# Small 32x32 products in the last step of a block inversion, and a later load of modulation weights

## The chip, the cores and the metric

The kernel runs on one core of a Trainium2 chip. The metric is device time in microseconds (us) of one execution, in which all weights are read from HBM.

## What is computed

The reference is a two-layer encoder trunk on 256 tokens of width 1024. Each layer has three sub-layers, each with a shift, a scale and a gate that are computed from a conditioning vector `c` (nine vectors of 1024 per layer, numbered 0 to 8 below):

```
for l in range(DEPTH):
    mod = cs @ ada_w[l] + ada_b[l]
    sh1, sc1, gt1, sh2, sc2, gt2, sh3, sc3, gt3 = jnp.split(mod, N_MOD, axis=-1)
    x = x + 0.5 * gt1 * swiglu(modulate(rmsnorm(x), sh1, sc1), ffn_wi[l, 0], ffn_wo[l, 0])
    x = x + gt2 * hybrid_mixer(modulate(rmsnorm(x), sh2, sc2), ...)
    x = x + 0.5 * gt3 * swiglu(modulate(rmsnorm(x), sh3, sc3), ffn_wi[l, 1], ffn_wo[l, 1])
```

The mixer has three branches of 8 heads of width 64: a dilated attention, a neighbourhood attention, and an RWKV-7 scan that runs once forward and once backward over the tokens. One step of the scan is

```
sa = jnp.einsum("dbhvk,dbhk->dbhv", state, a_vec)
state = state * w[..., None, :] + sa[..., None] * b_vec[..., None, :] + v[..., None] * k[..., None, :]
y = jnp.einsum("dbhvk,dbhk->dbhv", state, r)
```

## The kernel before, in words

**Dense products.** Every float32 weight tile is split into a high and a low part (ScalarE, line 374; VectorE, line 383), and each product of a 128x128 weight tile with 256 tokens is three matmuls (lines 418 to 420). This dense work is one thread of the program and goes on through all stages.

**The scan.** The tokens are cut into 4 chunks of 64, for both directions at once. Step n of `scan()` treats chunk n of the forward and chunk 3-n of the backward direction. Inside a chunk the recurrence becomes a triangular 64x64 system for each head and direction, and `invert()` computes its inverse (`TT`, and `T`, its transpose within 32x32 blocks). Two threads of `invert` run, one for chunks 0 and 2, one for 1 and 3; at most two chunks are held at a time, and a slot is given back when a step of the scan ends. For each chunk `invert` makes the products `pG` (line 1189), inverts the 8x8 diagonal blocks (`blocks8`: one matmul at line 1257, and 14 small VectorE operations at lines 1262 and 1266 between larger ones, the last at line 1269), and then joins blocks of 8, 16 and 32 in three levels. One level is: 16 products of 64x64 by 64x64 into `pX` (line 1213), a copy to SBUF (lines 863 or 865, on ScalarE or VectorE), 16 more into `pT` (line 1225), and a masked copy of the new corner blocks into `TT` (line 1227). After the levels 0 and 1 a VectorE transpose of 32x32 blocks (`flip`, line 1274) renews `T`. In the profile each of these float32 matmuls has two records, so 16 products are 32 records.

**After the scan.** Four `post` threads normalise its result, the last two write `oC` (lines 1486 to 1492), and the dense thread goes on with the product of `oC` and the third branch's weights, then with `w_out`.

**Modulations.** One block of the nine vectors (128 of their values) is a 512 KB load `araw` (issued by SyncE, line 509) and one VectorE multiply and sum over 128x1024 elements (line 482). When the dense work of FFN 1 has been ordered, `main` spawns the 24 blocks of the vectors 5, 7 and 6 with `ada(..., PACE, START)`: block i is loaded no earlier than START + PACE*i us later, by the planner's clock. They are read when `w_out` begins and in the next FFN.

**The order of the work.** No engine's order is written by hand. A planner (`Order`) runs all threads against a model of the engines, with a duration named at each `yield on(...)`, and emits the instructions in the order in which its model starts them; a changed duration or due time can move any instruction behind it. On the chip each engine then takes its instructions in that order. SBUF tiles come from a pool of 36 buffers, PSUM from 8 banks, and a thread that takes one waits until it is free.

Of the kernel before, what the change touches and what calls it, by code (L numbers as in the profile page):

```python
# [28 lines left out]
WARM = 0  # L29
NJ0 = 8  # L30
NXF, NXM = 4, 8
PACE, START = 7, 110
FPACE, FSTART = 5, 12
WPRIO = -1
LAT, MM = {"PE": 0.2, "ACT": 0.15, "DVE": 0.13, "SP": 0.0}, 0.329
# [122 lines left out]
def on(eng, dur, lat=None, tab=None):  # L158
    return ("on", eng, dur, LAT[eng if isinstance(eng, str) else eng[0]] if lat is None else lat, tab)


def wait(ev):
    return ("wait", ev, 0, 0)
# [6 lines left out]
def take(sem, n=1):  # L170
    return ("take", sem, n, 0)


def vec_t(n):
    return 0.07 + 1.04e-3 * n


def vec2_t(n):
    return 0.08 + 0.53e-3 * n


def act_t(n):
    return 0.05 + 0.83e-3 * n


def skew(a, b):

    return bass.AP(tensor=a.tensor, offset=a.offset, ap=[list(a.ap[0]), [b.offset - a.offset, 2]] + [list(x) for x in a.ap[1:]])
# [3 lines left out]
def trunk(ctx, tc, A, out):  # L192
    nc = tc.nc
    V, S_, P = nc.vector, nc.scalar, nc.tensor
# [7 lines left out]
    od = Order()  # L202
    s_raw, s_spl, s_ada = Sem(NRAW), Sem(NSPL), Sem(NADA)
    s_pm, s_px, s_big = Sem(NPM), Sem(8 - NPM), Sem(NBIG)
# [3 lines left out]
    def pmain():  # L208
        return ps.tile([128, 2, 256], F32, name="pmain", tag="bank", bufs=8)

    def paux(name, shape=(128, 512)):
        return ps.tile(list(shape), F32, name=name, tag="bank", bufs=8)

    def big(name, shape=(128, 4, S), dt=F32):
        return act.tile(list(shape), dt, name=name, tag="b4", bufs=NBIG)
# [7 lines left out]
    def free_big(n=1):  # L223
        od.release(s_big, n)
# [40 lines left out]
    for q in range(2):  # L265
        p = paux("pc")
# [7 lines left out]
    lvl = const.tile([128, 3, 2, 128], U8, name="lvl")  # L274
# [54 lines left out]
    for l in range(L):  # L329
# [3 lines left out]
        w = A["w_in"][l]  # L333
        gb = A["w_gb"][l]
        parts = {"a": (w, 8, 14), "b": (w, 14, 20), "c": (w, 0, 8), "A": (gb, 0, 6), "B": (gb, 6, 12), "g": (gb, 12, 16)}
        for q in ORDER:
            t, b0, b1 = parts[q]
# [498 lines left out]
    def half(h):  # L836
        return slice(64 * (h % 2), 64 * (h % 2) + 64)
# [22 lines left out]
    def copy_any(dst, src, n, f32=False):  # L860
        yield on(("ACT", "DVE"), (act_t(n), vec2_t(n) if f32 else vec_t(n)))
        if od.cur.pick == "ACT":
            S_.copy(dst, src)
        else:
            V.tensor_copy(dst, src)

    def mixer(l, st):
# [55 lines left out]
        def ar_view(d, q):  # L923
            return AR[d][q].rearrange("p (a b) t -> p a b t", a=2)
# [237 lines left out]
        def toks(c):  # L1162
            return slice(c * 64, c * 64 + 64)

        def invert(ns):
            for e in e_ab:
                yield wait(e)
            for n in ns:
                cs = (n, 3 - n)
                if n > 0:  # L1170
                    yield wait(e_got[n - 1])
                yield take(s_ck)
                for _ in range(3 + (n == ns[0])):
                    yield take(s_big)
                od.set(e_got[n])
                if n == ns[0]:
                    tx = big("tx", (128, 2, 2, 4, 64))
                    T, X = tx[:, 0], tx[:, 1]
                G = [big("G", (128, 2, 4, 128)) for _ in range(2)]
                tw = big("tw", (128, 2, 2, 4, 64))  # L1180
                TT, W1 = tw[:, 0], tw[:, 1]
                for d in range(2):
                    yield take(s_px, 2)
                    pp = [paux("pG", (128, 4, 128)) for _ in range(2)]
                    yield on("PE", 1.3)
                    for i in range(4):
                        for b in range(2):
                            hs = half(b)
                            P.matmul(pp[b][:, i], BK[d][i // 2][hs, i % 2, cs[d]].rearrange("p a b -> p (a b)"),  # L1189
                                     ar_view(d, i // 2)[hs, :, i % 2, toks(cs[d])], start=True, stop=True)  # L1190
                    for b in range(2):
                        yield on("DVE", 0.6)
                        V.tensor_mul(G[b][:, d], pp[b], mg[:, d][:, None, :].to_broadcast([128, 4, 128]))
                        od.release(s_px)
                yield from blocks8(G, X, TT)
                yield on("DVE", 0.6)
                flip(T, TT)
                od.spawn(values(n, cs, G, TT, W1), VPRIO)
                for lv in range(3):
                    w = 8 << lv  # L1200

                    def part_(t, d, a):
                        return t[:, d].rearrange("p h c -> p (h c)").rearrange("p (x a s) -> p x a s", a=2, s=w)[:, :, a]

                    def halves_(t, a):
                        return skew(part_(t, 0, a), part_(t, 1, 1 - a))

                    yield take(s_px)
                    px = paux("pX", (128, 2, 4, 64))
                    yield on("PE", 0.85)  # L1210
                    for d in range(2):
                        for h in range(8):
                            P.matmul(px[half(h), d, h // 2], G[h % 2][half(h), d, h // 2, 0:64], T[half(h), d, h // 2],  # L1213
                                     start=True, stop=True)
                    if lv == 0:
                        yield from copy_any(X, px, 512)
                    else:
                        yield from copy_any(halves_(X, 0), halves_(px, 0), 256)
                    od.release(s_px)
                    yield take(s_px)  # L1220
                    pt = paux("pT", (128, 2, 4, 64))
                    yield on("PE", 0.85)
                    for d in range(2):
                        for h in range(8):
                            P.matmul(pt[half(h), d, h // 2], X[half(h), d, h // 2], TT[half(h), d, h // 2], start=True, stop=True)  # L1225
                    yield on("DVE", 0.335)
                    V.copy_predicated(halves_(TT, 1), lvl[:, lv].rearrange("p d (x s) -> p d x s", s=w), halves_(pt, 1))
                    od.release(s_px)
                    if lv < 2:
                        yield on("DVE", 0.6)  # L1230
                        flip(T, TT)
                od.set(e_inv[n])
            free_big()

        def blocks8(G, m, TT):

# [35 lines left out]
        def flip(t, tt):  # L1272

            V.transpose(t.rearrange("p d a b -> p (d a b)"), tt.rearrange("p d a b -> p (d a b)"))
# [520 lines left out]
        for m in range(KT):  # L1795
            if m < NPM:
                p = p3[m]
                yield from dense(p, ma, KT, 4)
            else:
                yield take(s_pm)  # L1800
                p = pmain()[:, 0]
# [14 lines left out]
    def main():  # L1816
        st = first
        od.spawn(first_stats(st), -2)
        od.spawn(first_loads(), 0)
        od.spawn(late_consts(), 8)  # L1820
        od.spawn(weights(), WPRIO)
        od.spawn(weights_hi(), WPRIO)
        od.spawn(weights_lo(), WPRIO)
        for l in range(L):
            st = yield from ffn(l, 0, 0, st, [(l, 2), (l, 4), (l, 3)], (l, 1))
            od.spawn(ada([(l, 5), (l, 7), (l, 6)], 9, PACE, START), 9)
            st = yield from mixer(l, st)
            st = yield from ffn(l, 1, 2, st, [(l, 8), (l + 1, 1), (l + 1, 0)],
                                (l + 1, 0) if l + 1 < L else None)
        yield from rstd(st)  # L1830
        for k in range(KT):
            yield on("DVE", 0.34)
            V.tensor_mul(xT[:, k], xT[:, k], st.r)
            if k % 2 == 1 or k > 5:
                k0 = k - 1 if k < 6 else k
                nc.sync.dma_start(out[:, k0:k + 1], xT[:, k0:k + 1])
# [126 lines left out]
```

## Time and profile before

| | before |
|---|---|
| median of 3 runs | 1553.74 us (1552.37 to 1556.83) |
| profiled execution | 1554.94 us, span 1553.1 us |
| TensorE busy | 1508.4 us of the span (97%) |
| VectorE busy | 1282.1 us (83%) |
| ScalarE busy | 870.0 us (56%) |
| mean granted TensorE clock | 0.984 |

Busy times are unions of an engine's records, which overlap; a busy TensorE is therefore not one at its peak. PE is TensorE, PEld its weight loads, DVE VectorE, ACT ScalarE, SP SyncE. Times in the views count from the span's start. The mixer of layer 0 takes about 215 to 575 us, its scan about 415 to 555; the scan of layer 1 takes about 1160 to 1315.

### The profile page before, as it was taken

Reading aid. Unit: us, or ns where it says so; the run is one execution under the profiler, and the core shown is the slowest. Engines: PE = TensorE matmul, PEld = TensorE weight load, DVE = VectorE, ACT = ScalarE, POOL = GpSimd, SP = SyncE. Lnnn points to the kernel's source line nnn. Section 1 sums busy time; section 2 is a strip of 40 time slices with the busy share of each in tenths; the row PEclk is TensorE's granted clock in tenths of the full one; section 3 lists DMA queues with packets and bytes.
Section 4 is the critical chain, followed back from the end, with each engine's and each line's share of the span. In section 5 each row is a group of like instructions: output and inputs, shape, how many; then the busy total and the mean of one; then the engine's idle time right before and its main releaser. Section 6 shows DMA issues by size and latency. Waiting matters only on the chain.

```text
span 1553.1 us, 36366 instructions
## 1 busy us (share of the span) xinstructions
PE 1508.4 (97%) x14470; PEld 1438.6 (93%) x14470; DVE 1282.1 (83%) x2724; ACT 870.0 (56%) x1746; POOL 2.4 (0%) x22
## 2 busy tenths in 40 slices
PE   6999999999899999999999999999998999999997
PEld 6999999989688989999999999998887998999997
DVE  8888789989978688988789877899899785898664
ACT  4556467576444466554565555676654445665554
POOL 0000000000000000000000000000000000000000
PEclk8999999999999999999999999999999999999999
DMA  9688776547433445887667886654546433567553
GB/s 346 216 293 280 258 237 193 162 136 249 153 116 128 133 161 190 289 265 266 226 206 266 289 275 203 210 164 150 180 160 205 150 111 125 166 205 269 187 190 123
DMA packets 97377, 315.76 MB, mean 203 GB/s; under 512 B 11572, under 2 KB 23092, under 8 KB 97208
## 3 DMA queue, kind: packets, MB, share of 16 engines
q1 hardware_dynamic: 96920, 313.35, 60.2%
q8 instruction: 113, 1.85, 0.5%
q14 instruction: 56, 0.46, 0.1%
q10 hardware_dynamic: 288, 0.10, 0.0%
HBM read 310.27 MB, written 3.15 MB: 202 GB/s over the span
## 4 chain that ended last, share of the span: by engine, by line
PE 89%; DMA 4%; DVE 4%; issue 1%; ACT 1%; SPq 0%; DVEq 0%; ACTq 0%
PE pmain L418 21%; PE pmain L419 20%; PE pmain L420 20%; DMA araw<-in_ada_w_dram 3%; PE pearly L418 3%; PE pearly L419 2%; PE pearly L420 2%; PE pT L1225 1%; PE pX L1213 1%; PE pG L1189 1%; DVE wlo L383 1%; PE pfirst L419 1%; PE po L1582 1%; PE pfirst L420 1%; PE pfirst L418 1%
## 5 line engine op out<-in xcount | busy, mean ns | idle before, releaser
L374 ACT CAST whi<-wraw 128x512 fp32r<-128x512 f32 x828 | 508.5, 619 | 442.9 <-PE pmain L419 280.1
L383 DVE TENSOR_TENSOR wlo<-wraw,whi 128x512 fp32r<-128x512 f32 x828 | 566.2, 688 | 123.2 <-ACT whi L374 113.8
L418 PE MATMUL pmain<-h,whi 128*128 128x256 f32 x1840 | 531.1, 289 | 0.0
L420 PE MATMUL pmain<-h,wlo 128*128 128x256 f32 x1840 | 517.5, 281 | 0.7 <-DVE wlo L383 0.7
L419 PE MATMUL pmain<-h,whi 128*128 128x256 f32 x1840 | 516.8, 281 | 0.0
L418 PEld LDWEIGHTS pmain<-h,whi 128*128 128x128 f32 x1840 | 346.8, 188 | 13.8 <-issue 8.7
L419 PEld LDWEIGHTS pmain<-h,whi 128*128 128x128 f32 x1840 | 347.1, 189 | 1.3 <-issue 1.0
L420 PEld LDWEIGHTS pmain<-h,wlo 128*128 128x128 f32 x1840 | 346.8, 188 | 1.7 <-DVE wlo L383 1.5
L482 DVE CUSTOM_DVE_ANT_0 araw<-araw,csb 128x1024 f32<-128x1024 f32 x144 | 174.9, 1219 | 42.4 <-DMA araw<-in_ada_w_dram 42.0
L420 PE MATMUL pmain<-z,wlo 128*128 128x256 f32 x704 | 197.8, 281 | 5.2 <-DVE wlo L383 5.2
L419 PE MATMUL pmain<-z,whi 128*128 128x256 f32 x704 | 197.8, 281 | 0.0
L418 PE MATMUL pmain<-z,whi 128*128 128x256 f32 x704 | 197.2, 280 | 0.0
L420 PEld LDWEIGHTS pmain<-z,wlo 128*128 128x128 f32 x704 | 132.7, 188 | 6.2 <-DVE wlo L383 6.2
L419 PEld LDWEIGHTS pmain<-z,whi 128*128 128x128 f32 x704 | 132.7, 188 | 0.0
L418 PEld LDWEIGHTS pmain<-z,whi 128*128 128x128 f32 x704 | 132.5, 188 | 0.0
L418 PE MATMUL pearly<-xh,whi 128*128 128x258 f32 x320 | 91.5, 286 | 0.0
L419 PE MATMUL pearly<-xl,whi 128*128 128x258 f32 x320 | 90.4, 282 | 0.0
L420 PE MATMUL pearly<-xh,wlo 128*128 128x258 f32 x320 | 90.3, 282 | 0.0
L419 PEld LDWEIGHTS pearly<-xl,whi 128*128 128x128 f32 x320 | 60.6, 189 | 0.0
L420 PEld LDWEIGHTS pearly<-xh,wlo 128*128 128x128 f32 x320 | 60.5, 189 | 0.0
L418 PEld LDWEIGHTS pearly<-xh,whi 128*128 128x128 f32 x320 | 60.5, 189 | 0.0
L441 ACT CAST z<-ffz 128x256 fp32r<-128x256 f32 x76 | 30.6, 405 | 33.8 <-DVE ffz L673 33.2
(302 smaller groups left out, 2362.5 us busy)
## 6 DMA issues: line engine op xcount, KB each, us to landing
wraw<-in_ffn_wi_dram SPq DMA_DIRECT2D x160, 512.0 KB, 4.6
araw<-in_ada_w_dram SPq DMA_DIRECT2D x144, 512.0 KB, 6.2
wraw<-in_ffn_wo_dram SPq DMA_DIRECT2D x88, 512.0 KB, 4.7
wraw<-in_w_in_dram SPq DMA_DIRECT2D x78, 512.0 KB, 3.9
wraw<-in_w_gb_dram SPq DMA_DIRECT2D x72, 512.0 KB, 4.0
w0raw<-in_ffn_wi_dram SPq DMA_DIRECT2D x16, 512.0 KB, 10.9
wraw<-in_w_out_dram SPq DMA_DIRECT2D x16, 512.0 KB, 3.7
bt<-in_bt_dram SPq DMA_DIRECT2D x16, 192.0 KB, 5.0
```

The lines of the kernel that those rows point to most:

```text
L374: S_.copy(hi, part(q))
L383: V.tensor_tensor(lo, part(q), hi, op=OP.subtract)
L418: P.matmul(o, w[0], xh, start=first, stop=False)
L419: P.matmul(o, w[0], xl, start=False, stop=False)
L420: P.matmul(o, w[1], xh, start=False, stop=last)
L441: S_.copy(self.hi(k), src)
L482: V.tensor_tensor_reduce(out=raw, in0=raw, in1=csb, scale=0.5, scalar=0.0, op0=OP.mult, op1=OP.add, accum_out=modT[l][:, blk:blk + 1])
L1189: P.matmul(pp[b][:, i], BK[d][i // 2][hs, i % 2, cs[d]].rearrange("p a b -> p (a b)"), ar_view(d, i // 2)[hs, :, i % 2, toks(cs[d])], star ...
L1213: P.matmul(px[half(h), d, h // 2], G[h % 2][half(h), d, h // 2, 0:64], T[half(h), d, h // 2], start=True, stop=True)
L1225: P.matmul(pt[half(h), d, h // 2], X[half(h), d, h // 2], TT[half(h), d, h // 2], start=True, stop=True)
L1582: P.matmul(po[half(e)], vv[:, j, (2 * hp + e) * 64:(2 * hp + e + 1) * 64], pr_[:, 2 * e + j], start=j == 0, stop=j == 1)
```

## The change

The third level leaves the loop over levels (which is now `range(2)`, with a `flip` after each) and gets a code of its own. It computes for each head and direction one 32x32 block in place of a 64x64 one, and the blocks of both directions go into one PSUM region of 128 x 4 x 32. The planner's durations for its matmuls are 0.5 in place of 0.85. The loads of the vectors 5, 7 and 6 are paced by 4.5 us from 190 us on, in place of 7 us from 110 us on.

```diff
-PACE, START = 7, 110
+PACE, START = 4.5, 190
...
-                for lv in range(3):
+                for lv in range(2):
...
-                    if lv < 2:
-                        yield on("DVE", 0.6)
-                        flip(T, TT)
+                    yield on("DVE", 0.6)
+                    flip(T, TT)
+                yield take(s_px)
+                px = paux("pX", (128, 4, 32))
+                yield on("PE", 0.5)
+                corners(px, lambda d, i, b, k, ca, cb: G[b][k, d, i, cb], lambda d, i, k, ca, cb: T[k, d, i, ca], 1)
+                X2 = X[:, 0, :, 0:32]
+                yield from copy_any(X2, px, 128)
+                od.release(s_px)
+                yield take(s_px)
+                pt = paux("pT", (128, 4, 32))
+                yield on("PE", 0.5)
+                corners(pt, lambda d, i, b, k, ca, cb: X2[k, i], lambda d, i, k, ca, cb: TT[k, d, i, cb], 0)
+                yield on("DVE", 0.335)
+                V.copy_predicated(skew(TT[:, 0, :, 32:64], TT[:, 1, :, 0:32]), lvl[:, 2].rearrange("p d (x s) -> p d x s", s=32),
+                                  pt[:, None].to_broadcast([128, 2, 4, 32]))
+                od.release(s_px)
                 od.set(e_inv[n])
             free_big()
+
+        def corners(p, w, x, o):
+
+            for i in range(4):
+                for b in range(2):
+                    for d in range(2):
+                        A = slice(64 * b + 32 * d, 64 * b + 32 * d + 32)
+                        B = slice(64 * b + 32 - 32 * d, 64 * b + 64 - 32 * d)
+                        ca, cb = (slice(t.start - 64 * b, t.stop - 64 * b) for t in (A, B))
+                        to, k = (B, A) if o else (A, B)
+                        P.matmul(p[to, i], w(d, i, b, k, ca, cb), x(d, i, k, ca, cb), start=True, stop=True,
+                                 tile_position=(k.start, to.start))
```

## Rows read from the trace of the kernel before

**Rows 1.** The page, its parts 1 and 2.

```profile
PE 1508.4 (97%) x14470; PEld 1438.6 (93%) x14470; DVE 1282.1 (83%) x2724; ACT 870.0 (56%) x1746; POOL 2.4 (0%) x22
PE   6999999999899999999999999999998999999997
```

**Rows 2.** Windows, all engines: stretch, length, busy us (records), PEclk, DMA share, GB/s.

```profile
330.00:415.00 85.00, 80.54 (x610) 68.64 (x603) 77.33 (x181) 49.34 (x125) 0.00 (x0) 0.96 0.64 211
422.00:553.00 131.00, 130.96 (x2215) 119.39 (x2214) 99.05 (x214) 59.84 (x112) 0.00 (x0) 1.00 0.38 125
450.00:533.00 83.00, 83.00 (x1463) 75.76 (x1458) 65.03 (x138) 35.72 (x69) 0.00 (x0) 1.00 0.38 127
1095.00:1178.00 83.00, 80.30 (x668) 69.73 (x668) 77.69 (x177) 43.21 (x98) 0.00 (x0) 0.96 0.59 197
1178.00:1200.00 22.00, 19.59 (x419) 16.70 (x417) 19.56 (x51) 12.20 (x34) 0.00 (x0) 1.00 0.62 194
1200.00:1287.00 87.00, 87.00 (x1402) 79.44 (x1398) 66.94 (x141) 39.56 (x76) 0.00 (x0) 0.98 0.36 119
```

**Rows 3.** Timeline of PE: first matmuls after a wait; in brackets the idle time.

```profile
409.07 2.04 PE L1257 MATMUL p<-tx,c_b 128*128 128x512 f32 x2 [4.46 <-issue]
...
555.51 0.39 PE L418 MATMUL pmain<-oC,whi 128*128 128x256 f32 x1 [1.69 <-ACT oC L1490]
557.33 0.58 PE L419 MATMUL pmain<-oC,whi 128*128 128x256 f32 x1 [1.43 <-DVE oC L1492]
...
1169.73 1.15 PE L1213 MATMUL pX<-tx,G 64*64 64x64 f32 x32 [1.94 <-DVE tx L1274]
...
1187.38 1.15 PE L1213 MATMUL pX<-tx,G 64*64 64x64 f32 x32 [1.42 <-DVE tx L1274]
```

**Rows 4.** The chain that ended last: start, us, what; last inversion of layer 0.

```profile
529.58 1.08 PE pX L1213 x32
...
531.55 1.08 PE pT L1225 x32
...
533.89 1.08 PE pAS L1344 x32
```

**Rows 5.** The same chain, groups of float32 matmuls of other shapes (x = records).

```profile
251.79 0.87 PE pwz L991 x4
...
258.14 0.57 PE pkk L842 x8
...
331.02 1.06 PE pS L1542 x8
...
480.56 1.09 PE pG L1189 x16
```

**Rows 6.** Groups by form: the copies of pX, the masked copy; busy us, mean ns.

```profile
L863 ACT COPY tx<-pX 128x256 f32<-128x256 f32 x15 | 5.6, 372 | 18.4 <-PE pX L1213 18.4
L863 ACT COPY tx<-pX 128x512 f32<-128x512 f32 x7 | 4.1, 587 | 9.3 <-PE pX L1213 9.3
...
L1227 DVE COPY_PREDICATED tw<-lvl,pT 128x256 f32<-128x256 uint8 x24 | 10.5, 438 | 11.9 <-PE pT L1225 11.8
```

**Rows 7.** Windows, tile araw alone: stretch, length, DVE busy us (operations of line 482).

```profile
330.00:415.00 85.00, 12.10 (x10) 0.96 0.64 211
450.00:533.00 83.00, 12.09 (x10) 1.00 0.38 127
1095.00:1178.00 83.00, 8.55 (x7) 0.96 0.59 197
...
1200.00:1287.00 87.00, 12.66 (x11) 0.98 0.36 119
```

**Rows 8.** Timeline of SP: the first load of the 24 blocks in each layer.

```profile
334.65 0.45 SPq L509 DMA_DIRECT2D araw<-in_ada_w_dram  x1
...
1097.62 0.42 SPq L509 DMA_DIRECT2D araw<-in_ada_w_dram  x1
```

## The prediction

> **What bounds the kernel now.** I read the page first: TensorE is busy for 97% of the span, and no slice of the span but the first stands below 8 tenths [rows 1]. That alone does not say that shorter matmuls pay, because a busy TensorE may be waiting inside its pipeline. So I read windows of the two scans next. In layer 0 TensorE is busy for 130.96 of the 131 us between 422 and 553, at full clock, and in layer 1 for all of 1200 to 1287 [rows 2]: the dense thread fills every hole that the scan leaves, and a microsecond of scan matmuls taken away there is a microsecond that dense work moves up. The timeline of TensorE around these stretches shows what ends them [rows 3]. At the end of layer 0's scan TensorE waits 1.69 and 1.43 us for `oC`, so the dense work ran out a little before the scan's result was there: both ends lie close together, the scan's slightly behind. At the head it waits 4.46 us in layer 0 for the first `blocks8` and, among others, 1.94 and 1.42 us in layer 1 for the transposes of `T`. These waits are on VectorE, which is busy for 77.33 of 85 us before the scan of layer 0 and 77.69 of 83 before that of layer 1 [rows 2]. Last I read the chain of waits: the last inversion's third level is on it, 1.08 us for each of its two groups, and the scan's last step follows 1.3 us behind it [rows 4].
>
> **The third level's matmuls.** It has two groups of 16 products for each inversion, in 4 inversions of 2 layers: 16 groups. Now one takes 1.08 us [rows 4]. Its 32 records of 64 columns are 2048 columns. Other groups of 2048 columns take the same however many records they are: 1.06 us for 8 records of 256, 1.09 us for 16 of 128 [rows 5]. All of these use two parts of the array in turn. `pwz`, on one part, takes 0.87 us for 1024 columns, 0.85 ns a column; at that pace 2048 columns on two parts are 0.87 us, and some 0.2 us remain for entering and leaving the group. `pkk`, 2048 columns on four parts, takes 0.57 us: 0.435 for the columns and 0.135 over. The new group has 32 records of 32 columns, 1024 in all, on four parts that share neither rows nor columns: 0.22 us for the columns and 0.135 to 0.2 around them, 0.35 to 0.42. No row has records as dense as 32 in 0.22 us, so I take 0.45. The dearest bound is no overlap of the four, 0.87 + 0.2 = 1.07, and 0.2 more where such a group meets one of the other shape: 1.29. The saving is 0.63 us a group, **10.1 us in all, 5.0 a layer**; its ends are +11.7 (0.35) and -3.4 (1.29).
>
> Here the Trainium skill speaks against the change: TensorEngine Tiling (Array Packing), in Restrictions and Gotchas, says that different row tiles cannot access the same PSUM bank at once, and all four parts here write one bank. By that rule the sum would lose its 10.1 us. The trace disagrees for two parts: `pX` before the change is two row parts writing one bank, and its 2048 columns take 1.08 us where one part after the other would need 1.74. For four row parts no row here shows it.
>
> **The rest of that level.** The copy of `pX` shrinks from 256 to 128 columns; a line through 372 ns at 256 and 587 at 512 gives 265 [rows 6]. On ScalarE, 56% busy, the 0.1 us is hidden, on the scan's chain it counts. The masked copy still writes 256 elements, and I leave it at 438 ns [rows 6]; it may fall to half if the repeated source were what it is paid for, which I don't assume. The transposes stay three for an inversion. One inversion is thus 2 x 0.63 + 0.1 = 1.4 us shorter from end to end. Two stand in series in each layer, as chunk 3 waits for a slot that chunk 1's scan step gives back: **2.7 us a layer on the chain**.
>
> **The later loads.** START moves by 80 us, so the 24 blocks that begin at 334.65 and 1097.62 us [rows 8] begin near 415 and 1178 and, 4.5 apart, are all issued near 518 and 1281. What moves with a block is the issue and the wait for a buffer on SyncE, the 512 KB, and 1.21 us of VectorE (12.10 for 10) [rows 7]. All 10 blocks leave 330 to 415 and all 7 leave 1095 to 1178, 12.1 and 8.55 us of VectorE in its fullest stretches. What that gives is bounded by nothing and by the waits of the scans' heads, 4.46 and 3.36 us; I take about half, **2.0 us a layer**, since other VectorE work stands before those operations too. In exchange the scan gets more: with 5 to 6 us to land, about 17 blocks fall in 450 to 533 where 10 do now, and about 19 in 1200 to 1287 where 11 do, 7 and 8 more, 8.5 and 9.7 us. VectorE is busy 65.03 of 83 and 66.94 of 87 us there, so it has room for them, but it takes its work in order, and one that stands before an operation of `blocks8` or before a flip holds the scan back by up to its own length. The ends are nothing and all of it. I take a quarter, **2.3 us a layer**: the chain is on TensorE for about half of its way, and idle VectorE absorbs half of the rest. The bytes cost nothing there (DMA share 0.38), and a weight load queued on SyncE behind a block's wait for a buffer is covered by the tiles already split, as no wait for a weight stands in that stretch, TensorE being busy for 130.96 of 131 us; if the cover went, what is late next is the dense thread's next tile.
>
> **The sum.** Seen from TensorE, a layer ends 5.0 + 2.0 = 7.0 us earlier. Seen from the scan's chain it is 2.7 + 2.0 - 2.3 = 2.4. The chain is the later one at the end, but its matmuls stand in TensorE's queue between dense ones and gain from each that is gone, so I take the middle, 4.7 a layer, 9.4 in two. The profiled execution took 1554.94 us (span 1553.1); less 9.4 that is 1545.5. The median of the runs, 1553.74, lies 1.2 lower, so on that scale the forecast is **1544.3 us**.
>
> **The rivals.** *First, the four parts do not overlap*, be it for the bank or because 32 records cannot be issued that fast. Then a group takes 1.07 to 1.29 us, TensorE gains 0 to -3.4, the loads net -0.3 a layer, and the time is 1554 to 1558. For it: no row has four row parts. Against it: the two that pair now. Chance 0.08. This is also the case that the change does not do what it says. *Second, the end of the scan eats the gain*: TensorE's time is saved, dense work runs out earlier, and the wait for `oC`, 3.1 us now [rows 3], grows by what was saved, because `post` and its ScalarE work come in a new order. Then 1551 to 1554. For it: the scan's end is already the later. Chance 0.15. *Third, slower: the modulations' VectorE work stands in the scan's chain.* Place: `blocks8` and the flips of the last two inversions. Price: 8.5 + 9.7 = 18 us if all is on the chain, against the chain's gains of 2 x (2.7 + 2.0) = 9.4; it decides from the point where more than half of the added work delays the chain, and with all of it the time is 1563. For it: the 14 small operations are separate places in a queue in order. Against it: over 18 us of idle VectorE in each of these stretches. Chance 0.15. *Fourth, better*: the waits at both heads and ends go, a layer gains 5.0 + 3.4 to 4.5 + 3, about 11 to 12, and the time is near 1531. Chance 0.12.
>
> **How the numbers follow.** The forecast has 0.5: its own range is 2 x 2.4 to 2 x 7.0 us of gain, 1540 to 1549. About 0.3% (4.7 us) is what a measurement of this kernel can tell from no change. Faster by more: the forecast, the fourth rival, less a small part of the forecast that falls short: 0.61. Within: the second rival, half of the first, that part: 0.22. Slower: the third and some of the first: 0.17. The range reaches from 1533, short of the whole of the fourth rival, to 1557, which takes in most of the first and the milder half of the third.
>
> **What would show it.** In the changed profile the third level's groups keep 32 records each, of 32 columns, and should take 0.35 to 0.5 us from their start to the next group's; at 1 us or more the first rival is right. The stretch from the first inversion to `oC` should be some 5 us shorter in each layer, with TensorE still full in it. No operation on `araw` should stand between 330 and 410 or 1095 and 1175, and the wait before the first `blocks8` matmul of layer 0 should be about half. A longer wait for `oC` speaks for the second rival; more time from the `blocks8` matmul to the first level's products in the late inversions, with line 482 between, for the third. Wrong it would also be if the new order of the plan opened waits that no row here has, above all at the start of the next FFN, which reads the vectors that now arrive later.

## The result, and the profile after

The changed kernel takes **1535.78 us** (1534.15 to 1540.22, 4 runs) against 1553.80 before (4 runs): ratio 0.9888, 95% interval 0.9870 to 0.9907. It is 18.0 us faster, on the forecast side and inside the range, but about twice the 9.4 us of the sum, and faster than the 1540 to 1549 that the forecast gave as its own range. The profiled execution took 1537.14 us, its span is 1535.3.

The page of the changed kernel, parts 1 and 2, beside [rows 1]:

```profile
PE 1495.0 (97%) x14470; PEld 1424.6 (93%) x14470; DVE 1283.9 (84%) x2731; ACT 859.4 (56%) x1735; POOL 2.3 (0%) x22
PE   6999999999999989999999999999999998999998
```

TensorE's busy time fell by 13.4 us for the same number of records; its share stayed. The 8 that stood in the eleventh slice (388 to 427 us, the head of layer 0's scan) is a 9 now, and an 8 has come in the fifteenth, where that scan ends; in layer 1 it moved likewise, from the thirty-first to the thirty-fourth.

Windows of the changed kernel, all engines, beside [rows 2] (the columns are the same):

```profile
330.00:415.00 85.00, 85.00 (x705) 73.44 (x706) 75.80 (x185) 50.93 (x123) 0.00 (x0) 1.00 0.43 141
...
450.00:533.00 83.00, 82.29 (x1386) 75.28 (x1383) 71.61 (x153) 35.58 (x68) 0.00 (x0) 1.00 0.55 182
...
1095.00:1178.00 83.00, 82.92 (x910) 70.43 (x912) 72.48 (x178) 46.39 (x110) 0.00 (x0) 1.00 0.42 138
```

The chain that ended last, in the changed kernel, beside [rows 4], and the same groups with the tile `pX`:

```profile
524.77 0.38 PE pX L1258 x32
...
526.04 0.38 PE pT L1258 x32
...
528.39 1.08 PE pAS L1370 x32
```

```profile
L1258 PE MATMUL pX<-tx,G x256: 191/191/212, 422.9 to 1271.2; 32*32 32x32 f32 x128
L863 ACT COPY tx<-pX x18: 266/374/590, 412.0 to 1271.5; 128x512 f32<-128x512 f32 x7, 128x128 f32<-128x128 f32 x6, 128x256 f32<-128x256 f32 x5
```

A group of the third level still has 32 records and takes 0.38 us where it took 1.08; the copy of 128 columns takes 266 ns (265 was forecast).

The blocks of modulations (windows with tile `araw`, beside [rows 7]) and the waits of TensorE (timeline, beside [rows 3]) in the changed kernel:

```profile
330.00:415.00 85.00, 0.00 (x0) 1.00 0.43 141
450.00:533.00 83.00, 18.25 (x15) 1.00 0.55 182
1095.00:1178.00 83.00, 0.00 (x0) 1.00 0.42 138
1200.00:1280.00 80.00, 18.28 (x15) 1.00 0.56 193
```

```profile
392.80 1.02 PE L1283 MATMUL p<-tx,c_b 128*128 128x512 f32 x2
...
544.75 1.97 PE L1489 MATMUL pgi<-c_ident,gsq 128*128 128x128 f32 x8 [3.25 <-DVE gsq L1484]
550.11 0.58 PE L418 MATMUL pmain<-oC,whi 128*128 128x256 f32 x1 [3.40 <-ACT oC L1516]
...
553.28 0.58 PE L419 MATMUL pmain<-oC,whi 128*128 128x256 f32 x1 [0.46 <-DVE oC L1518]
```

No block is left before the scans. The first `blocks8` matmul of layer 0 stands at 392.80 where it stood at 409.07, and the wait of 4.46 us before it is gone altogether. In its place layer 0's scan ends with waits of 3.25, 3.40 and 0.46 us where there were 1.69, 1.43 and 0.33.

Where the time came from, by the start of the last matmul on `oC` in each layer and of the last matmul of FFN 1 in layer 1, in the profiled executions:

| profiled execution | last on `oC`, layer 0 | FFN 1 of layer 1 ends | last on `oC`, layer 1 | mixer of layer 1 |
|---|---|---|---|---|
| before | 571.9 | 975.9 | 1332.4 | 356.5 |
| changed | 566.2 | 969.8 | 1314.5 | 344.7 |
| later loads alone | 569.2 | 972.3 | 1322.1 | 349.8 |
| small products alone | 567.7 | 969.5 | 1320.3 | 350.8 |

Layer 0 up to the end of its scan gave 5.7 us, layer 1's mixer 11.8; the rest of the program gave 0.3. The two parts divide differently: the small products alone gave 4.2 and 5.7 us, the later loads alone 2.7 and 6.7. Each row is one execution, and FFN 1 of layer 0, which no edit touches, ends between 213.8 and 216.1 us in these four. Counted from there, the first column gives 5.9 us to the whole change, 5.4 to the products and 1.6 to the loads.

### The profile page after: what moved, and what is told of

Same layout as the page of the kernel before. It is cut to its first block, busy times and chain, and to the rows that moved or that the text cites. A ratio compares the mean times of both kernels' runs of the same rounds, so it can differ in the third digit from the quotient of the medians.

```text
span 1535.3 us, 36372 instructions
## 1 busy us (share of the span) xinstructions
PE 1495.0 (97%) x14470; PEld 1424.6 (93%) x14470; DVE 1283.9 (84%) x2731; ACT 859.4 (56%) x1735; POOL 2.3 (0%) x22
## 4 chain that ended last, share of the span: by engine, by line
PE 89%; DMA 5%; DVE 3%; issue 1%; SPq 1%; ACT 0%; DVEq 0%; ACTq 0%
PE pmain L418 21%; PE pmain L419 20%; PE pmain L420 20%; DMA araw<-in_ada_w_dram 3%; PE pearly L418 3%; PE pearly L420 2%; PE pearly L419 2%; DVE wlo L383 1%; PE pT L1225 1%; PE pX L1213 1%; PE pS L1568 1%; PE po L1608 1%; PE pfirst L419 1%; PE pmain L1724 1%; PE pfirst L420 1%; PE pfirst L418 1%
```

## The experiments

**The two parts alone.** Each kernel has one part of the change. The first:

```diff
-PACE, START = 7, 110
+PACE, START = 4.5, 190
```

> The kernel before with the new PACE and START alone; all products 64x64. Theory (the two parts add: 16 groups of matmuls that went from 1.08 to 0.38 us give 11.2 us, the later loads the remaining 7): 1547, between 1544 and 1550, with the wait before the first blocks8 matmul of layer 0 gone. Rival one (the small products give all, the loads nothing): 1552 to 1556. Rival two (the loads give most of it): below 1543.

Measured: 1545.51 us (1542.92 to 1547.82), ratio 0.9949 (0.9936 to 0.9961): 7.9 us faster than the 1553.42 of its runs before. The second is the changed kernel with

```diff
-PACE, START = 4.5, 190
+PACE, START = 7, 110
```

> The changed kernel with PACE and START as before; the third level of 32x32 products stays. Theory: 1542.6, between 1540 and 1546, and the waits at the heads of both scans about as before. Rival one (the products give all): 1534 to 1538. Rival two (the loads give most): 1547 or more.

Measured: 1543.11 us (1540.21 to 1545.72), ratio 0.9930 (0.9917 to 0.9944): 10.3 us faster. The two together make 18.2, and the whole change made 18.0: the parts add as far as the intervals can tell, and both rivals that give all to one of them fall. The first `blocks8` matmul of layer 0 in these two, from the timeline of TensorE, first the loads alone, then the products alone:

```profile
391.03 1.02 PE L1257 MATMUL p<-tx,c_b 128*128 128x512 f32 x2
```

```profile
410.44 2.04 PE L1283 MATMUL p<-tx,c_b 128*128 128x512 f32 x2 [4.46 <-issue]
```

The wait at the head belongs to the loads: they remove it, the products leave it at 4.46 us. After that wait the two records take twice as long, at half clock (0.50 of full).

But the head of layer 0 is not where the loads' gain lies. In the kernel with the loads alone the first matmul on `oC` of layer 0 starts at 555.1 us, where it started at 555.5: between 530 and 560 us TensorE is idle for 8.1 us in place of 3.5, at a granted clock of 0.72 in place of 0.95. VectorE's timeline shows one reason, a block that stands ahead of the last `post` operations and waits for its load:

```profile
546.56 1.22 DVE L482 CUSTOM_DVE_ANT_0 araw<-araw,csb 128x1024 f32<-128x1024 f32 x1 [4.69 <-DMA araw<-in_ada_w_dram]
```

Most of the gain is in layer 1's mixer. There TensorE's waits for the flips, 4.7 us before, are gone and those for `oC` are 2.3 us longer; and its busy time is 4.0 us shorter for the same matmuls, at a mean granted clock of 0.99 for 0.98.

**The products in another order.** The same 16 products of a group, four in a row to one part of the array; every engine has the same lines in the same order as in the changed kernel.

```diff
-            for i in range(4):
-                for b in range(2):
-                    for d in range(2):
+            for b in range(2):
+                for d in range(2):
+                    for i in range(4):
```

> The changed kernel with the loops of the third level turned round, so that four products in a row go to one part of the array; every engine's order of lines is the same. Theory (the time of a group is its columns over the parts that overlap): a group takes 0.9 to 1.1 us in place of 0.38, and since TensorE is full there the run is 8 to 11 us slower than the changed kernel, 1544 to 1547. Rival (TensorE's time in the scan is covered by the scan's own chain): groups as long, but less than 4 us slower.

Measured: 1541.51 us (1536.56 to 1543.54), ratio 0.9920 (0.9906 to 0.9934), 5.7 us slower than the changed kernel's 1535.78, where 8 to 11 were expected. Its chain:

```profile
525.05 0.82 PE pX L1258 x32
...
526.76 0.82 PE pT L1258 x32
```

A group takes 0.82 us for the same 1024 columns, a little under the 0.9 that was expected, so TensorE has 16 x 0.44 = 7.0 us more to do. Some 5 to 6 of them reach the total (5.0 by the ratios, 5.7 by the medians). This shows that the group's time comes from the four parts overlapping. How much of TensorE's time in the scans counts it shows only roughly: three quarters by these figures, but the two intervals allow from about 1 us to more than the whole 7.0.

**The second level in small products too.** The changed kernel with 32 products of 32x32 on the four diagonal parts for level 1.

```diff
+                    if lv == 1:
...
+                        px = paux("pX", (128, 2, 4, 32))
+                        yield on("PE", 0.65)
+                        diagonal(px, lambda d, i, b, k, c: G[b][k, d, i, c], lambda d, i, k, c: T[k, d, i, c])
...
+                        for c in range(2):
+                            V.copy_predicated(skew(TT[:, 0, :, 32 * c + 16:32 * c + 32], TT[:, 1, :, 32 * c:32 * c + 16]),
...
```

> The changed kernel with the second level, too, in 32x32 products on four parts: 32 of them in place of 16 of 64x64, two masked copies of 128 elements in place of one of 256. A group should take 16 steps of 32 ns and 0.13 around them, 0.64 us, for 1.08: 16 groups, 7.0 us of TensorE, and 0.1 to 0.2 us more of VectorE for each of 8. Theory (TensorE's time counts): 1528 to 1531. Rival (the wait for oC at the end of the scan, already longer in the changed kernel, takes it): 1534 to 1538.

Measured: 1538.54 us (1536.80 to 1539.90), ratio 0.9904 (0.9891 to 0.9917): no faster than the changed kernel. Fourteen of the 16 new groups take 0.68 us, a little over the 0.64, and TensorE's busy time fell by another 5.3 us to 1489.7, but the rest of its span grew from 40.3 to 46.7 us: it waits longer for the scan's end. Layer 1 in the timeline of TensorE:

```profile
1295.75 1.11 PE L1520 MATMUL pgi<-c_ident,gsq 128*128 128x128 f32 x4 [4.85 <-DVE gsq L1515]
1298.27 0.58 PE L418 MATMUL pmain<-oC,whi 128*128 128x256 f32 x1 [1.41 <-ACT oC L1547]
...
1302.32 0.58 PE L419 MATMUL pmain<-oC,whi 128*128 128x256 f32 x1 [1.78 <-DVE oC L1549]
```

At the end of that scan the changed kernel waits 4.8 us in all, this one 8.3. Here the second rival of the prediction holds: the dense work has run out, and a shorter group only lengthens the waits at the scan's end.

**What the loads' VectorE operations cost.** Two kernels, the one before and the changed one, in which the sum over a block of the vectors 5, 6 and 7 runs over 64 of its 1024 columns. Loads, planned durations and every engine's order stay.

```diff
-        yield on("DVE", 1.14)
-        V.tensor_tensor_reduce(out=raw, in0=raw, in1=csb, scale=0.5, scalar=0.0, op0=OP.mult, op1=OP.add,
+        w = slice(0, 64 if blk // 8 in (5, 6, 7) else D); yield on("DVE", 1.14)
+        V.tensor_tensor_reduce(out=raw[:, w], in0=raw[:, w], in1=csb[:, w], scale=0.5, scalar=0.0, op0=OP.mult, op1=OP.add,
```

> The kernel before, with the VectorE operation of the 48 moved blocks cut from 1024 to 64 columns (it leaves out most of the sum of these three vectors); their loads and every engine's order stay. Theory (the later loads gained because VectorE's 1.2 us a block no longer stands in the stretches before the scans): the 4.46 us wait before the first blocks8 matmul shrinks to under 2 us, and the run gains as much as the later loads alone did or more: 1540 to 1547. Rival (it was the new order of the plan, or the bytes): 1551 to 1555.

Measured: 1550.00 us (1546.19 to 1553.76), ratio 0.9979 (0.9968 to 0.9990): 2.8 us by the medians, 3.3 by the ratio, of the 7.9 that the later loads give. VectorE's busy time in 330 to 415 us falls from 77.33 to 69.36, and yet the wait at the head of layer 0's scan does not shrink. (The matmul stands 3 us later than before; FFN 1 ends 2.2 us later here, at 217.1.)

```profile
412.05 2.05 PE L1257 MATMUL p<-tx,c_b 128*128 128x512 f32 x2 [4.47 <-issue]
```

The theory falls: 4.47 us of wait for 4.46, though 8 us of VectorE's work ahead of it are gone. VectorE's timeline of the kernel before shows why. No operation of line 482 runs between 397.7 us and that matmul. From 404.5 us on VectorE works without a break on the scores of an attention and on the operations that `blocks8` makes ahead of its matmul. The last one of `blocks8` ends at 408.97, and the matmul starts 0.1 us later:

```profile
408.28 0.69 DVE L1251 TENSOR_TENSOR tx<-w,c_d 128x512 f32<-128x512 f32 x1
```

So the wait, for which the profile names no releaser, is one for VectorE, as the prediction read it, but not for the sums. What the short sums gain is in layer 1, whose mixer takes 352.5 us for 356.5; the waits for the flips there fall from 4.7 to 2.4 us. In the changed kernel:

> The changed kernel with the same cut; loads and order stay. It prices what these operations cost where they stand now. If their length delays the scan's chain: 5 us or more faster than the changed kernel, below 1531. If what delays the end of layer 0's scan is that one of them waits there for its load to land, with the post operations behind it in VectorE's queue: 1 to 4 us, 1532 to 1535, and the wait for oC in layer 0 stays above 2 us. If they cost nothing there: 1535 to 1537.

Measured: 1534.67 us (1529.50 to 1535.96), ratio 0.9872 (0.9852 to 0.9892), against 0.9888 for the changed kernel: 1 to 2.5 us, which the intervals cannot tell from nothing. At the end of layer 0 the wait for `gsq` falls from 3.25 to 1.46 us; that for `oC` stays:

```profile
543.90 1.97 PE L1489 MATMUL pgi<-c_ident,gsq 128*128 128x128 f32 x8 [1.46 <-DVE gsq L1484]
...
549.30 0.58 PE L418 MATMUL pmain<-oC,whi 128*128 128x256 f32 x1 [3.44 <-ACT oC L1516]
```

So the length of these operations is not what holds `oC` there. VectorE's timeline in the changed kernel shows what stands there:

```profile
546.75 0.42 DVE L1512 TENSOR_TENSOR rkv<-rkv,pgi 128x256 f32<-128x256 f32 x1
547.72 1.23 DVE L482 CUSTOM_DVE_ANT_0 araw<-araw,csb 128x1024 f32<-128x1024 f32 x1 [0.54 <-DMA araw<-in_ada_w_dram]
548.87 0.08 DVE L482 DVE_READ_ACCUMULATOR2_ANT modT<- 128x1 f32 x1
548.87 0.42 DVE L1518 TENSOR_TENSOR oC<-rkv,oC 128x256 fp32r<-128x256 f32 x1
```

A block's sum stands between two operations that make `oC` and waits 0.54 us for its own load; line 1518 has to wait behind both. With the sum cut short the same operation waits 1.58 us, and line 1518 starts no sooner after line 1512, 2.2 us in place of 2.1:

```profile
547.91 0.23 DVE L482 CUSTOM_DVE_ANT_0 araw<-araw,csb 128x64 f32<-128x64 f32 x1 [1.58 <-DMA araw<-in_ada_w_dram]
```

It is the landing of the load that sets the time here.

**The order that the later loads bring.** The kernel before with the later loads *and* the short sums:

```diff
-PACE, START = 7, 110
+PACE, START = 4.5, 190
...
+        w = slice(0, 64 if blk // 8 in (5, 6, 7) else D); yield on("DVE", 1.14)
...
```

> e1_loads_only (the kernel before with the later loads) with the VectorE operations of the 48 blocks cut to 64 columns, as in e5_before_short_sums. The two differ now only in when the blocks are loaded and in the order that the plan gives all work. If the new order is what the later loads bring (the first pG of layer 0 stood at 392.6 us and stands at 378 with them): this one is 5 to 9 us faster than e5, 1541 to 1545. If the gain of the later loads is VectorE's time alone: within 2 us of e5, 1548 to 1552.

Measured: 1541.57 us (1537.64 to 1545.08), ratio 0.9924 (0.9908 to 0.9941). It is 8.4 us faster than the short sums with the early loads, and has no wait at the head:

```profile
394.62 1.02 PE L1257 MATMUL p<-tx,c_b 128*128 128x512 f32 x2
```

With hardly any VectorE time in the sums the later loads still give their 8 us; and the short sums give as much with the later loads (about 3.9 us by the ratios, against the later loads alone) as with the early ones (3.3). So the later loads' gain is not that the sums have moved. What is left is the new order and the times of the loads. With the 24 blocks due later, the planner has `pG` of layer 0 start at 378.0 us (381.6 in this kernel) in place of 392.6, and the matmul after it no longer holds up TensorE's queue. In the profiles, though, the gain is again in layer 1: its mixer takes 345.6 us here and 352.5 with the early loads, while the last matmul on `oC` of layer 0 stands at 572.7 and 573.5. Which of the new places in layer 1 makes the difference is not shown. That the bytes alone, in another order, would do nothing was not tried; order and load times move together here.

**Where the loads should stand.** The changed kernel with three other values of START.

```diff
-PACE, START = 4.5, 190
+PACE, START = 4.5, 160
```

> The changed kernel with START 160 in place of 190 (PACE 4.5). Theory (in layer 0 the last blocks stand in VectorE's queue between the operations that make oC): no operation of line 482 after the last scan step of layer 0, the wait for oC there under 2 us, and 1531 to 1534. Rival (the blocks are back in the stretch before the scan and the head gets later by what the end gains): 1535 to 1539.

Measured: **1530.57 us** (1528.47 to 1531.77), ratio 0.9852 (0.9832 to 0.9871), faster than both kernels. With 175:

> The changed kernel with START 175 (PACE 4.5). If TensorE's half clock at the end of layer 0's scan (0.55 of full in 545 to 560 us in the changed kernel, 1.00 with START 160) is what START 160 gained there: it goes with the last operations of line 482 in that stage; if some of them still stand between those of post, half clock stays and the time is 1533 to 1537, else 1528 to 1532.

Measured: 1531.28 us (1526.34 to 1532.96), ratio 0.9856 (0.9839 to 0.9873). With 130:

> The changed kernel with START 130 (PACE 4.5). If the loads' place is a balance between the scan's head and its end: waits for the flips at the heads of both scans as in e7_start_160 or longer, no wait at the end of layer 0's scan, 1533 to 1540. If earlier is simply better with the faster pace: 1526 to 1531.

Measured: 1539.34 us (1538.92 to 1540.83), ratio 0.9915 (0.9904 to 0.9927). The end of layer 0's scan, windows of all engines, for the changed kernel, START 160 and START 175 in turn:

```profile
536.00:560.00 24.00, 16.71 (x140) 14.92 (x139) 18.20 (x43) 8.86 (x19) 0.00 (x0) 0.64 0.46 160
```

```profile
536.00:560.00 24.00, 24.00 (x206) 24.00 (x205) 21.90 (x49) 15.11 (x30) 0.00 (x0) 1.00 0.66 227
```

```profile
536.00:560.00 24.00, 20.44 (x138) 19.21 (x139) 20.69 (x51) 11.36 (x23) 0.00 (x0) 0.79 0.37 130
```

With START 160 no block is left there, TensorE is full at full clock, and a price is paid at the head of layer 0: waits for the flips in the timeline of TensorE, of which the changed kernel has one, of 0.7 us.

```profile
409.78 1.15 PE L1213 MATMUL pX<-tx,G 64*64 64x64 f32 x32 [2.47 <-DVE tx L1300]
...
420.43 1.15 PE L1213 MATMUL pX<-tx,G 64*64 64x64 f32 x32 [2.93 <-DVE tx L1300]
```

With START 175 one block (1.22 us) still stands between the operations of `post`, and the clock stays partly low, at 0.79; the expectation tied that to 1533 to 1537, yet the time is that of START 160. So the clock at this place is not shown to be what START 160 gained. With START 130 both scans have waits for the flips in their heads, and layer 1 a wait of 4.5 us before a `blocks8` matmul; but layer 0 also waits 2.6 us for `oC` at its end, which was not expected, although no block stands there. Of the four values 190 is too late and 130 too early; 160 and 175 can't be told apart. That this is a balance between a scan's head and its end is in part argued, since each value also gives every queue a new order.

**Both at once.** The second level in small products, with START 160:

```diff
-PACE, START = 4.5, 190
+PACE, START = 4.5, 160
```

> The second level in 32x32 products as in e4_level1_small, with START 160. If the blocks at the end of layer 0's scan were what took that version's gain: 1527 to 1532. If the scan's own end (post, its ScalarE tables) takes it in both layers: 1533 to 1538.

Measured: 1546.13 us (1540.41 to 1551.71), ratio 0.9953 (0.9937 to 0.9968): worse than either edit alone, and than every expectation. The time goes into waits for the flips in layer 0, for the operations before `oC` at the ends of both layers, and into a kind that the other kernels hardly have: stops of TensorE inside a group. The longest waits of TensorE in layer 1, engine and line, what was waited for, us in total, times, longest:

```profile
PE pT L1277 <- issue: 4.6, 3, 2.5
PE pgi L1520 <- DVE gsq L1515: 3.9, 1, 3.9
PE pX L1289 <- issue: 1.5, 1, 1.5
```

## Why the prediction was right, and what was mis-sized

The direction was right, and so was the mechanism of the products. The number lies inside the stated range, but between the forecast's own range and the fourth rival. Of the 9.4 us of the sum, the middle of its two views, the products are 7.7 and the loads 1.7; measured alone, they give 10.3 and 7.9. Most of what was missing comes from the loads, by a way that the prediction did not have, so that the whole stayed inside the range is in part luck.

**The products: right in kind, close in size, too cheaply passed on.** The new group was put at 0.45 us and took 0.38, inside the bounds of 0.35 and 1.29; 11.2 us of TensorE for the 10.1. (The upper bound's own terms, 1.07 and 0.2, make 1.27; nothing hangs on it.) The reasoning by columns held: 1024 columns on four parts. The first rival fell. The rule that the prediction weighed, that row tiles cannot share a PSUM bank at once (the Trainium skill, TensorEngine Tiling (Array Packing), Restrictions and Gotchas), would have cost all of it; in these runs four row parts write disjoint partitions of one bank, and the group shows no such price (0.38 us, against 0.82 with the parts in turn). The step that failed is the sum: it took the middle between TensorE's view (5.0 a layer) and the chain's (2.7). The part alone gives 10.3 us, what TensorE's view said, and undoing its overlap costs 5 to 6 of 7.0. TensorE's view was the better one while dense work lasted. Once the changed kernel had used that up, it failed: with the second level made small, another 5.3 us of TensorE bought nothing.

**The later loads: a term was missing.** The prediction set 2.0 us a layer gained at the heads against 2.3 lost in the scans, and 1.7 us of it reached the sum; alone they give 7.9 us. Both terms were priced as VectorE time that stands before other work. The short sums show that this time is worth 3.3 us in the kernel before, over both layers, and 3.9 in the one with the loads alone: moving it nets little, as the prediction's 2.0 against 2.3 had it. What it left out is the new order with the new load times, 8.4 us at short sums. The front part of the document says that a changed due time can move any instruction behind it; the prediction gave this no term and no rival with a gain. The head's wait of 4.46 us, which I halved because VectorE was 91% busy before it, does not hang on the sums: it stays at 4.47 without them and goes with the new order. And its going brought layer 0 little, since the waits at the end of that layer grew.

**The slower rival, and the second.** More blocks do stand in the scans now, 15 operations in 450 to 533 us where there were 10 and the prediction had 17. Cutting all 48 short gains 1 to 2.5 us, not clear of nothing, where the added work alone was priced at 4.6. What the third rival missed is where they hurt: not in `blocks8` but behind the last scan step of layer 0, where one waits for its landing. The second rival was named with 0.15, and part of it came true: waits of 7.1 us in all at the end of layer 0 where 3.5 were. That is part of why that layer gave 5.7 us and the other 11.8; START 160, without these waits, brings the last matmul on `oC` there to 560.6 us from 566.2.

**The signs named ahead.** 32 records a group: right. Groups of 0.35 to 0.5 us: right. No block before the scans: right. The wait before `blocks8` halved: it went. TensorE still full in the scans: 82.29 of 83 us, right until their ends. New waits at the start of the next FFN: none.

Two signs failed. The stretch from the first inversion to `oC` should have been some 5 us shorter in each layer. From the first `blocks8` matmul to the first one on `oC` it is 157.3 us in layer 0 for 146.4, and 159.2 in layer 1 for 161.4: in layer 0 the new order brings the first of these forward by 16.3 us and the second by only 5.4. And the sign of the third rival came without the rival: in layer 0 the third inversion takes 20.1 us from its `blocks8` matmul to its first product, with four sums between, where it took 14.6 with one. With the sums cut short it is still 19.4, so it is not their length.

## What to carry to other kernels

Where an engine is full because a filler thread takes every hole, most of its time saved is total time saved, until the filler ends before the chain it fills; look for how far apart the two ends are before shortening the engine's work once more. The small matmuls here are priced by columns over the parts of the array that overlap, and the loop order has to give neighbours different parts. In a kernel ordered by a planner a due time is an edit of every queue: price it by experiment with the order held, as the short sums did, and look in every stage for what it moved: here it removed the most visible wait, and gained its time elsewhere. Place background loads so that no engine waits for one between the operations that end a stage.

## What was not expected of the hardware

**The clock after the waits at layer 0's end.** In the changed kernel the granted clock is 0.64 of full over 536 to 560 us, and 0.55 over the window 545 to 560; before the change it is 0.94 over the former stretch, and 0.88 over 560 to 575, where its matmuls on `oC` stand. TensorE waited 3.25 us, ran 8 records of `pgi`, and waited 3.40 again, and the matmuls on `oC` that follow run at the lower of the two levels, 1.2 GHz. With START 160, without these waits, the clock stays at 1.00, and the mixer's dense work ends earlier although the first matmul on `oC` starts at nearly the same time, 549.3 us for 550.1. Here the two waits cost more than their own length.

**Stops inside dense groups.** In the two kernels with the second level in small products TensorE stops inside a group of 32x32 products, for nothing that the profile shows: once, 0.50 us, with START 190, and four times, 0.45, 1.54, 2.48 and 1.63 us, with START 160, 6.1 us in all. The longest, in the timeline of TensorE of that kernel:

```profile
1241.84 0.70 PE L1277 MATMUL pT<-tw,tx 32*32 32x32 f32 x58
1245.02 0.32 PE L1277 MATMUL pT<-tw,tx 32*32 32x32 f32 x6 [2.48 <-issue]
```

Three of the four are in groups of 64 records, one in a group of 32. In all other kernels a float32 group outside the dense work stops in this way at most once in a profile, for 0.26 to 0.34 us. What the engine waits for stays open; no run separates the supply of instructions from other causes.
